# Two chained transformer blocks on one core: later norm statistics, halved conditioning products, plain float32 for the small heads

## The chip, the cores and the metric

The kernel runs on one core of a Trainium2 chip. The metric is device time in microseconds (us), smaller is better. A core has TensorE (PE; its weight loads are shown as PEld), VectorE (DVE), ScalarE (ACT), GpSimd (POOL), and SyncE (SP), which here only starts DMA transfers. Each engine runs its own instructions in order and waits on semaphores for the others.

## The reference, cut to what matters

Two blocks run one after the other on 256 tokens of width 1024. The first is a hybrid block of two layers on a latent and a context stream of 256 tokens each. Each layer begins with a conditioning vector: a product of one row per stream with `w_ada`, which scales and shifts the norm.

```
shift, scale, gate = split((silu(c) @ w_ada + b_ada), 3)      # and the same for the context
h = rmsnorm(x, norm_w) * (1 + scale) + shift
```

The second block also has two layers. Layer 0 mixes with `mixer_ab`, layer 1 with `mixer_cd`; both then do a cross-attention to a memory of 256 tokens and a gated feed-forward (`swiglu`, 2816 wide).

```
mixer_ab: qa, ka, va, qb, kb, vb = split(h @ w_in)       # 8 query heads, 2 key/value heads, 64 wide, twice
          a: rms_norm(q), rms_norm(k), rope, softmax(q k^T / 8) v
          b: rope, window mask, a sink column in the softmax
mixer_cd: c: compressed heads: q, k 64 + 32 wide, 8 heads, softmax(q k^T / sqrt(96)) v
          d: near heads: 8 heads, 64 wide, with a bias table and a column mask
every mixer, the cross-attention and the feed-forward read rms_norm(x) of the residual x
```

## The kernel before, in words

Activations lie feature-major, 128 features by 256 tokens per tile (`x[:, k]`, k from 0 to 7). A float32 operand is cut into a high and a low part in the reduced type fp32r (`split`, L266): ScalarE rounds (`copy`), VectorE subtracts. A product is then three matmuls (`mm3`, L258). Weights come as pieces of 128 x 1024 floats (512 KB) over SyncE's DMA queue into `w_raw` (three buffers), ScalarE makes `w_high`, and VectorE or GpSimd makes `w_low` (`split_into`, L250). Which of the two does it is set by the table `POOL` (L34): for each part of the program the first number says every how many pieces one goes to GpSimd, 0 for none. Ab has 1 (all), cd has 3.

Heads of 64 features use another form (`mm_stacked`): high and low parts of q are stacked over 128 rows, and k is laid twice, once high over high, once low over zeros (`stack_q`, `stack_k`), so a product is two matmuls. The softmax (`softmax_t`) takes scores of two heads in one PSUM bank: VectorE takes the maximum, ScalarE exponentiates and sums, VectorE scales (L1299), TensorE transposes, and the result is split into two parts again. `pair_values` (L1312) multiplies it with the values, three matmuls per product, 64 or 128 output rows.

The statistics of a norm: ScalarE squares each residual tile, GpSimd (VectorE for the last) sums the squares into `acc`. `rstd_cols` sums `acc` over the partitions with a matmul against ones (L347) and VectorE runs eleven small instructions for the inverse root (`rsqrt`, L331); `rstd_unit` lays the result along a row with two more products (L357) and a copy. The projections themselves read the unscaled tiles (`raw_norm`), and the factor is applied to their results. So the statistics are needed only behind a projection, though the program states them ahead of it.

The conditioning: `ada_product` (L502) computes 512 columns of one layer's row from eight pieces of k, loaded two at a time in four loads; each product has 32 output rows and takes one of four column groups of the array, and the second half of k is added onto the first in PSUM.

The order: the first block is traced inside a block that a planner schedules by a simulated timeline. The second block is ordered by the same framework by priority, which follows the order of the program, and by when operands are ready; so the order on an engine is not that of the lines. Loads are issued on SyncE in the order in which buffers come free. PSUM has eight banks: three `mm`, two `sc`, two `tp`, one `pv`.

## Time and profile before

| | us |
|---|---|
| median of 3 runs | 2439.83 (2437.66 to 2440.39) |
| the profiled execution | 2442.6 |
| its span | 2440.8 |
| TensorE busy in it | 2296.8 (94%) |
| VectorE busy | 1617.7 (66%) |
| ScalarE busy | 1163.4 (48%) |
| GpSimd busy | 472.2 (19%) |
| ab output projection, 1797 to 1829: TensorE busy | 31.7 of 32 |
| first feed-forward, 1878 to 2062: TensorE busy | 183.8 of 184 |
| second layer up to 2101, from 2062: TensorE busy | 36.0 of 39 |
| median from issue to landing of a 512 KB weight load | 3.4 |

Rows of the profile give times in us from the start of the span unless marked ns. A row of the order of time has the start, the duration, the engine, the line of the kernel, the operation, the tiles (out<-in), the shape and the count of what was merged; in brackets the idle time of the engine before it, and what ended it. A plain float32 matmul is recorded as two matmuls, a transpose or a reduced one as one. Matmuls are pipelined, so the distance of starts, and not the duration, tells what one takes of TensorE. PEclk is the granted clock as a share of full speed (2.4 GHz; the other level is 1.2 GHz).

The second block begins at about 1663 (mixer ab to 1829, with the memory's keys and values inside it, cross to 1867, feed-forward to 2062, mixer cd to 2200, cross, feed-forward to 2432).

### The profile page before, as it was taken

To read this page: it belongs to the slowest core of one execution; us is meant where nothing else is said; L and a number is where in the kernel's file an instruction comes from. 1 tells how busy PE (TensorE), PEld (TensorE's weight loads), DVE (VectorE), ACT (ScalarE), POOL (GpSimd) and SP (SyncE) were. 2 spreads that over 40 slices of the span, in tenths; PEclk is the share of its full clock that TensorE was granted. 3 is DMA by queue.
4 is the path that set the end of the run, shared out by engine and by line. 5 is a ranking of instruction groups with operands and counts; after the bars stand their busy time and mean duration, and the time that the engine had idled before them with its cause. 6 is when DMAs were issued, how large, how long until landed. Compare 5 with 4: busy or idle time off the path is not lost.

```text
span 2440.8 us, 40377 instructions
## 1 busy us (share of the span) xinstructions
PE 2296.8 (94%) x15566; PEld 2066.6 (85%) x15566; DVE 1617.7 (66%) x3372; ACT 1163.4 (48%) x2172; POOL 472.2 (19%) x354
## 2 busy tenths in 40 slices
PE   6999999999999999989999999898698999888998
PEld 3787878798797887779889999896588999788998
DVE  5745566466575555586557778666987766887765
ACT  3344443444554233335445666444465444665543
POOL 2422220111121102002110000123352211222221
PEclk8999999999999999999999999998899999999999
DMA  6223234323323434443445434554233555433554
GB/s 254 78 92 114 95 109 155 125 88 101 116 93 131 151 103 154 142 130 117 134 147 186 131 113 141 180 166 147 86 102 123 183 183 180 132 109 121 189 183 139
DMA packets 111072, 330.87 MB, mean 136 GB/s; under 512 B 12320, under 2 KB 24352, under 8 KB 110880
## 3 DMA queue, kind: packets, MB, share of 16 engines
q1 hardware_dynamic: 90432, 299.87, 37.5%
q10 hardware_dynamic: 20448, 28.42, 3.4%
q8 instruction: 123, 2.02, 0.4%
q14 instruction: 69, 0.57, 0.1%
HBM read 309.36 MB, written 18.87 MB: 134 GB/s over the span
## 4 chain that ended last, share of the span: by engine, by line
PE 80%; DVE 12%; ACT 3%; DMA 3%; issue 2%; POOL 0%; ACTq 0%; SPq 0%; DVEq 0%; POOLq 0%
PE mm L262 22%; PE mm L263 22%; PE mm L264 22%; PE pv L262 2%; PE pv L263 2%; PE pv L264 2%; DVE w_low L257 1%; DVE h L274 1%; ACT w_high L256 1%; DVE e L1299 1%; DMA w_raw<-wstream 1%; PE mm L510 1%; PE sc L303 1%; DVE mx L1279 1%; PE sc L304 1%
## 5 line engine op out<-in xcount | busy, mean ns | idle before, releaser
L256 ACT CAST w_high<-w_raw 128x1024 fp32r<-128x1024 f32 (+1 forms) x490 | 508.0, 1038 | 583.1 <-PE mm L263 351.8
L257 DVE TENSOR_TENSOR w_low<-w_raw,w_high 128x1024 fp32r<-128x1024 f32 (+1 forms) x395 | 497.3, 1260 | 189.3 <-ACT w_high L256 184.8
L262 PE MATMUL mm<-big,w_high 128*128 128x512 f32 (+1 forms) x1664 | 573.3, 346 | 12.4 <-DVE g L942 5.7
L263 PE MATMUL mm<-big,w_high 128*128 128x512 f32 (+1 forms) x1664 | 571.3, 344 | 0.0
L264 PE MATMUL mm<-big,w_low 128*128 128x512 f32 (+1 forms) x1664 | 570.0, 343 | 0.0
L257 POOL TENSOR_TENSOR w_low<-w_raw,w_high 128x1024 fp32r<-128x1024 f32 x95 | 230.4, 2428 | 739.6 <-ACT w_high L256 600.3
L262 PEld LDWEIGHTS mm<-big,w_high 128*128 128x128 f32 x1664 | 316.1, 190 | 56.6 <-DVE g L942 6.1
L264 PEld LDWEIGHTS mm<-big,w_low 128*128 128x128 f32 x1664 | 316.4, 190 | 37.5 <-DVE w_low L257 0.4
L263 PEld LDWEIGHTS mm<-big,w_high 128*128 128x128 f32 x1664 | 316.6, 190 | 36.5 <-DVE big L271 0.2
L263 PE MATMUL mm<-w_low,big 128*128 128x256 f32 x960 | 269.9, 282 | 4.2 <-POOL w_low L257 2.8
L262 PE MATMUL mm<-w_high,big 128*128 128x256 f32 x960 | 268.0, 282 | 1.6 <-ACT w_high L256 1.6
L264 PE MATMUL mm<-w_high,big 128*128 128x256 f32 x960 | 268.3, 281 | 0.0
L263 PE MATMUL mm<-h,w_high 128*128 128x256 f32 x896 | 255.5, 285 | 4.8 <-DVE h L274 4.1
L262 PE MATMUL mm<-h,w_high 128*128 128x256 f32 x896 | 253.4, 284 | 2.7 <-ACT h L273 1.7
L264 PE MATMUL mm<-h,w_low 128*128 128x256 f32 x896 | 253.6, 283 | 0.0
L263 PEld LDWEIGHTS mm<-w_low,big 128*128 128x128 f32 x960 | 181.1, 189 | 6.2 <-POOL w_low L257 3.7
L262 PEld LDWEIGHTS mm<-w_high,big 128*128 128x128 f32 x960 | 180.6, 189 | 3.5 <-ACT w_high L256 2.8
L264 PEld LDWEIGHTS mm<-w_high,big 128*128 128x128 f32 x960 | 181.0, 189 | 0.4
L263 PEld LDWEIGHTS mm<-h,w_high 128*128 128x128 f32 x896 | 169.7, 189 | 7.6 <-DVE h L274 7.5
L262 PEld LDWEIGHTS mm<-h,w_high 128*128 128x128 f32 x896 | 169.5, 190 | 4.4 <-ACT h L273 2.8
L264 PEld LDWEIGHTS mm<-h,w_low 128*128 128x128 f32 x896 | 169.7, 190 | 0.1
L1649 POOL TENSOR_TENSOR x<-x,r 128x256 f32<-128x256 f32 x44 | 60.2, 1368 | 190.7 <-ACT t L1648 190.7
(475 smaller groups left out, 4388.8 us busy)
## 6 DMA issues: line engine op xcount, KB each, us to landing
w_raw<-wstream SPq DMA_DIRECT2D x486, 512.0 KB, 3.4
w_raw<-wstream SPq DMA_DIRECT2D x32, 448.0 KB, 3.2
big<-wstream SPq DMA_DIRECT2D x16, 512.0 KB, 9.0
gates<-y ACTq DMA_DIRECT2D x24, 256.0 KB, 2.0
w<-gates SPq DMA_DIRECT2D x18, 256.0 KB, 3.8
load<-yacc ACTq DMA_DIRECT2D x16, 256.0 KB, 3.0
yacc<-w ACTq DMA_DIRECT2D x12, 256.0 KB, 2.0
gates<-y ACTq DMA_DIRECT2D x24, 128.0 KB, 1.8
```

Source lines behind the costliest of these rows:

```text
L256: nc.scalar.copy(h, raw)
L257: eng.tensor_tensor(lo, raw, h.bitcast(F32), op=ALU.subtract)
L262: nc.tensor.matmul(out, a[0], b[0], start=start, stop=False)
L263: nc.tensor.matmul(out, a[0], b[1], start=False, stop=False)
L264: nc.tensor.matmul(out, a[1], b[0], start=False, stop=stop)
L274: nc.vector.scalar_tensor_tensor(lo, src, scale, h.bitcast(F32), op0=ALU.mult, op1=ALU.subtract)
L303: nc.tensor.matmul(out, q, k[0], start=start, stop=False)
L304: nc.tensor.matmul(out, q, k[1], start=False, stop=stop)
L510: nc.tensor.matmul(ps[j:j + 32], self.sc32[:, 2 * q + k], raw[:, k], start=(q < 2), stop=(q >= 2))
L1279: nc.vector.reduce_max(mx, ps2, axis=AX.X, negate=True)
L1299: nc.vector.tensor_scalar(p[:, u], p[:, u], sm[:, u:u + 1], None, op0=ALU.mult)
L1649: nc.gpsimd.tensor_tensor(g, g, rb, op=ALU.mult)
```

## The change

- `POOL`: parts ab and cd give no weight split to GpSimd any more.
- The heads of 64 and of 96 features are computed in plain float32: queries and keys are copied once (keys into halves of tiles that are zero elsewhere, `make_zeroed_halves`, `key_tile`), probabilities are copied once, values are laid between zeros (`between_zeros`, two GpSimd memsets per tile), and the two heads of a pair add into one bank. A score product is one matmul instead of two or three, a value product one instead of three. The cross-attention keeps the three-matmul form.
- `rstd_cols` (and `rstd_unit`) stand behind the first projection of ab, cd, cross and feed-forward.
- The conditioning is made in two halves of k, one per head: four products after two loads, the last loaded one first and at high priority, the other three ordered behind it. The first half is copied to `acc`, the second added to it by VectorE.
- Tile counts follow: `act` 16 to 8, `p` 4 to 3, `vz` 4 new; the first eight feed-forward results use `vz`.

```diff
@@ -28,11 +28,11 @@
...
-SECOND = dict(load=2, act=16, q=8, p=4, x=4, e=3, s=2, t=3, r=2)
+SECOND = dict(load=2, act=8, vz=4, q=8, p=3, x=4, e=3, s=2, t=3, r=2)
...
-            merge0=(0, 0), merge1=(0, 0), t=(4, 2), e=(0, 0), ab=(1, 0), x=(3, 2), cd=(3, 1), f=(0, 0))
+            merge0=(0, 0), merge1=(0, 0), t=(4, 2), e=(0, 0), ab=(0, 0), x=(3, 2), cd=(0, 0), f=(0, 0))
@@ -296,6 +296,15 @@
...
+            self.zero_tiles.append(t)
+
+    def make_zeroed_halves(self, n):
+
+        self.zero_tiles, self.n_zero = [], 0
+        for i in range(n):
+            t = [self.pool.tile([P, S], F32, tag=f"kz{i}{u}", name=self.name("kz"), bufs=1) for u in range(2)]
+            for u in range(2):
+                self.nc.gpsimd.memset(t[u][64 * (1 - u):64 * (2 - u)], 0.0)
@@ -495,21 +504,26 @@
...
-    def ada_group(self, l, groups):
-        for g in groups:
-            self.ada_product(l, g)
-
-    def ada_product(self, l, g):
+    def ada_half(self, l, g, half):
...
-        for q in range(4):
-            raw = self.raw_weights("w_ada", l, 2 * q, 2, _cols(512 * g, 512)).rearrange("p (k c) -> p k c", k=2)
-            for k in range(2):
-                j = 32 * (2 * (q % 2) + k)
-                nc.tensor.matmul(ps[j:j + 32], self.sc32[:, 2 * q + k], raw[:, k], start=(q < 2), stop=(q >= 2))
+        raw = [self.raw_weights("w_ada", l, 4 * half + 2 * q, 2, _cols(512 * g, 512)).rearrange("p (k c) -> p k c", k=2) for q in range(2)]
+
+        def product(j):
+            return nc.tensor.matmul(ps[32 * j:32 * j + 32], self.sc32[:, 4 * half + j], raw[j // 2][:, j % 2], start=True, stop=True)
+
+
+        with self.tc.high_priority():
+            first = product(3)
+            with self.tc.issue_after(first.ins if hasattr(first, "ins") else first):
+                for j in range(3):
+                    product(j)
+        if half == 0:
+            nc.scalar.copy(self.acc, ps)
+            return
...
-        nc.scalar.copy(row, ps)
+        nc.vector.tensor_tensor(row, ps, self.acc, op=ALU.add)
@@ -676,8 +690,7 @@
...
-            if hd in (1, 3):
-                self.ada_group(l, range(4 + hd // 2, 5 + hd // 2))
+            self.ada_half(l, 4 + hd // 2, hd % 2)
@@ -689,9 +702,9 @@
...
+                if l == 0:
+                    self.ada_half(1, pair, u)
...
-            if l == 0:
-                self.ada_group(1, range(pair, pair + 1))
@@ -1300,7 +1313,9 @@
...
-        if whole:
+        if not isinstance(pts, tuple):
+            nc.scalar.copy(pts[:, :, :, sl], pt)
+        elif whole:
@@ -1309,16 +1324,28 @@
...
-    def pair_values(self, y, k, pts, vs):
-
-        po = self.bank("pv").rearrange("p (u c) -> p u c", u=2)
+    def between_zeros(self, n):
+
+        v = self.u("vz", [P, 64 * (2 * n + 1)])
+        self.nc.gpsimd.memset(v[:, :P * n].rearrange("p (g c) -> p g c", c=P)[:, :, :64], 0.0)
+        self.nc.gpsimd.memset(v[:, P * n:], 0.0)
+        return v, v[:, 64:].rearrange("p (g c) -> p g c", c=P)[:, :, :64]
+
+    def pair_values(self, y, k, pts, v, heads):
+
+        po = self.bank("pv")[:, :S]
...
-            m = 64 * (u + 1)
+            lo = P * heads[u] + 64 * (1 - u)
...
-                vh, vl = vs(u, s)
-                self.mm3(po[:m, u], (vh, vl), (pts[0][:, u, s], pts[1][:, u, s]), s == 0, s == 1)
-            rows = slice(64 * u, 64 * u + 64)
-            self.split(y[0][rows, k, :S], y[1][rows, k, :S], po[rows, u])
+                self.nc.tensor.matmul(po, v[s][:, lo:lo + P], pts[:, u, s], start=u == 0 and s == 0, stop=u == 1 and s == 1)
+        self.split(y[0][:, k, :S], y[1][:, k, :S], po)
+
+    def key_tile(self, src):
+
+        k = self.zeroed()
+        for u in range(2):
+            self.nc.scalar.copy(k[u][64 * u:64 * u + 64], src[64 * u:64 * u + 64])
+        return k
@@ -1366,37 +1393,32 @@
+        tab = {nm: self.cst(nm).rearrange("p (t c) -> p t c", t=2) for nm in ("r1_c", "r1_s", "r2_c", "r2_s")}
+
+        pss = self.tok_wide("w_in_ab_2", 0, h, AB_KV, self.early)
         r = self.rstd_cols(self.acc[:, :S], S, D)
-        tab = {nm: self.cst(nm).rearrange("p (t c) -> p t c", t=2) for nm in ("r1_c", "r1_s", "r2_c", "r2_s")}
-
-        pss = self.tok_wide("w_in_ab_2", 0, h, AB_KV, self.early)
...
-            v = tuple(self.u("act", dt=F32R) for _ in range(2))
-            vsrc = pss[t][:, 256:].rearrange("p (g c) -> p g c", c=64)
-            for dup in range(2):
-                o = [x.rearrange("p (g u c) -> p g u c", u=2, c=64)[:, :, dup] for x in v]
-                self.split(o[0], o[1], vsrc, scale=r[:, t:t + 1])
+            v, at = self.between_zeros(4)
+            nc.scalar.activation(at, pss[t][:, 256:].rearrange("p (g c) -> p g c", c=64), AF.Copy, scale=r[:, t:t + 1])
             vv.append(v)
...
+            kr = self.u("x")
+            kv = kr.rearrange("p (g u c) -> p g u c", u=2, c=64)
+            for i, (kx_, rn) in enumerate(((ka, "r2"), (kb, "r1"))):
+                self.rope_tok([kv[:, 2 * i + g, 0].unsqueeze(1) for g in range(2)], kx_, tab[rn + "_c"][:, t], tab[rn + "_s"][:, t], 2, 32)
+                nc.scalar.copy(kv[:, 2 * i:2 * i + 2, 1], kv[:, 2 * i:2 * i + 2, 0])
...
+        kT = [[self.key_tile(src[:, g * S:(g + 1) * S]) for g in range(2)] for src in (kt_ps, kt_ps2)]
@@ -1426,62 +1448,50 @@
-                qT[kind].append([self.u("q", dt=F32R) for _ in range(2)])
-                for u in range(2):
-                    self.stack_q(qT[kind][i][u], ptq[i][64 * u:64 * u + 64])
+                qT[kind].append(self.u("q"))
+                nc.scalar.copy(qT[kind][i], ptq[i])
...
-                        self.mm_stacked(ps[:, u], qT[kind][pr // 2][u][:, qsl], tuple(x[:, ksl] for x in kT[kind]), kind == 0, kind == 0 or u == 1)
+                        nc.tensor.matmul(ps[:, u], qT[kind][pr // 2][:, qsl], kT[kind][g][u], start=kind == 0, stop=kind == 0 or u == 1)
                     self.softmax_t(ps, pts, qi, sink=[x[:, 2 * pr:2 * pr + 2] for x in sink] if kind else None)
...
+            if j == 0:
+                q = self.u("q")[:, :S]
+                self.nc.vector.tensor_tensor(q, ps, rb, op=ALU.mult)
+            else:
+                k = self.zeroed()
+                for u in range(2):
+                    sl = slice(64 * u, 64 * u + 64)
+                    self.nc.vector.tensor_tensor(k[u][sl], ps[sl], rb[sl], op=ALU.mult)
+        return q, k
...
-        r = self.rstd_cols(self.acc[:, :S], S, D)
-        rb = self.rstd_unit(r)
@@ -1492,11 +1502,14 @@
...
                 ps = self.feat(w, 0, h, 0, S)
+                if lo == 0 and j == 0:
+                    r = self.rstd_cols(self.acc[:, :S], S, D)
+                    rb = self.rstd_unit(r)
                 nc.vector.tensor_tensor(raw[:, j], ps, rb, op=ALU.mult)
...
             rc = self.rstd_rows(acc, S, n * P, by=96.0 if n == 2 else 1.0)
-            c = tuple(self.u("p", [P, 2, S], F32R) for _ in range(2))
+            c = tuple(self.u("q", [P, 2, S], F32R) for _ in range(2))
             self.norm_gain(c, raw, rc, [self.vec(gain, k) for k in range(n)], "t")
@@ -1559,20 +1572,18 @@
...
-                a, b = (self.u("q", [P, 2, S], F32R)[:96] for _ in range(2))
-                self.split(a, b, pt)
-                pair.append((a, b))
-            pts = self.new_pts()
+                a = self.u("q", [P, 2, S])[:96]
+                nc.scalar.copy(a, pt)
+                pair.append(a)
+            pts = self.u("p", [P, 2, 2, S])
...
-                    a, b = pair[u]
-                    qsl = slice(qi * P, (qi + 1) * P)
-                    self.mm3(ps[:, u], (a[:, 0, qsl], b[:, 0, qsl]), (a[:, 1], b[:, 1]), True, True)
+                    nc.tensor.matmul(ps[:, u], pair[u][:, 0, qi * P:(qi + 1) * P], pair[u][:, 1], start=True, stop=True)
...
-            self.pair_values(y, pr, pts, lambda u, s, pr=pr: tuple(x[:, P * pr:P * pr + 64 * (u + 1)] for x in vc[s]))
-
-            pts = self.new_pts()
+            self.pair_values(y, pr, pts, vc, (2 * pr, 2 * pr + 1))
+
+            pts = self.u("p", [P, 2, 2, S])
@@ -1608,6 +1616,10 @@
+            if pr == 0:
+                r = self.rstd_cols(self.acc[:, :S], S, D)
+                rs = self.small("x_rs", [P, 2])
+                nc.vector.tensor_scalar(rs, r[:, :2], 128.0 ** -0.5, None, op0=ALU.mult)
@@ -1635,13 +1647,14 @@
...
-        rb = self.rstd_unit(self.rstd_cols(self.acc[:, :S], S, D))
...
+            if f == 0:
+                rb = self.rstd_unit(self.rstd_cols(self.acc[:, :S], S, D))
@@ -1649,7 +1662,9 @@
...
-            a = self.u("act" if f < 16 else "q", [P, 2, S], F32R)
+            if f % 2 == 0 and f < 8:
+                two = self.u("vz", [P, 2, 2, S], F32R)
+            a = two[:, f % 2] if f < 8 else self.u("act" if f < 16 else "q", [P, 2, S], F32R)
...
```

## Rows read from the trace of the kernel before

**Rows 1.** The stretches of time: start:end, length, busy time and count per engine, PEclk, DMA.
```profile
0.00:1663.00 1663.00, 1589.73 (x10236) 1398.58 (x10236) 1053.24 (x2363) 755.87 (x1402) 270.64 (x222) 0.99 0.40 132
1663.00:1740.00 77.00, 56.43 (x223) 44.17 (x223) 56.34 (x125) 30.93 (x53) 28.99 (x12) 0.80 0.37 124
1740.00:1797.00 57.00, 45.11 (x291) 39.24 (x291) 53.17 (x128) 37.56 (x113) 16.75 (x8) 0.94 0.18 56
...
2101.00:2176.00 75.00, 62.65 (x442) 56.24 (x442) 64.25 (x125) 57.96 (x152) 17.27 (x14) 0.93 0.37 120
```

**Rows 2.** TensorE's waits from 1663 to 1740: total us, times, longest.
```profile
PE tp L1426 <- DVE x L1337: 7.7, 2, 7.5
PE tp L1394 <- DVE x L1337: 4.9, 1, 4.9
...
PE tp L347 <- DVE acc L379: 2.7, 1, 2.7
```

**Rows 3.** TensorE's waits from 1740 to 1797.
```profile
PE tp L1301 <- DVE e L1299: 8.2, 7, 1.9
```

**Rows 4.** VectorE in order of time, in the first key norm of ab.
```profile
1681.78 0.16 DVE L337 SCALAR_TENSOR_TENSOR hn_r_t<-hn_r_y 128x2 f32<-128x2 f32 x1
1681.97 2.36 DVE L338 TENSOR_TENSOR hn_r_t<-hn_r_t,hn_r_v 128x2 f32<-128x2 f32 x1
```

**Rows 5.** GpSimd in order of time: memsets ahead of ab, and one weight split.
```profile
1641.47 1.92 POOL L298 MEMSET kz<- 64x512 f32 x4
...
1681.95 2.37 POOL L257 TENSOR_TENSOR w_low<-w_raw,w_high 128x1024 fp32r<-128x1024 f32 x1 [0.43 <-ACT w_high L256]
```

**Rows 6.** Groups on GpSimd from 1663 to 1829: count, busy us, mean ns, idle before.
```profile
L257 POOL TENSOR_TENSOR w_low<-w_raw,w_high 128x1024 fp32r<-128x1024 f32 x26 | 62.4, 2403 | 98.6 <-ACT w_high L256 89.3 <-DMA load<-rpb 5.6 <-PE pv L264 3.8
```

**Rows 7.** Groups on VectorE from 1663 to 1829.
```profile
L1299 DVE TENSOR_SCALAR e<-e,sm 128x256 f32<-128x256 f32 x32 | 20.1, 663 | 0.2
L274 DVE SCALAR_TENSOR_TENSOR h<-xres,vecs,h 128x256 fp32r<-128x256 f32 x15 | 17.9, 1225 | 3.9 <-ACT h L273 3.9
...
L271 DVE TENSOR_TENSOR p<-tp,p 128x512 fp32r<-128x512 f32 x16 | 10.7, 682 | 1.4 <-ACT p L270 1.3
L338 DVE TENSOR_TENSOR hn_r_t<-hn_r_t,hn_r_v 128x8 f32<-128x8 f32 x6 | 7.5, 1252 | 0.2
```

**Rows 8.** Groups on VectorE from 2062 to 2200.
```profile
L257 DVE TENSOR_TENSOR w_low<-w_raw,w_high 128x1024 fp32r<-128x1024 f32 x17 | 22.1, 1298 | 3.2 <-ACT w_high L256 3.1
```

**Rows 9.** TensorE in order of time: two reduced matmuls of 256 columns.
```profile
1745.24 0.28 PE L303 MATMUL sc<-act,q 128*128 128x256 f32 x1
1745.36 0.28 PE L304 MATMUL sc<-kz,q 128*128 128x256 f32 x1
```

**Rows 10.** TensorE in order of time, the statistics in the first feed-forward.
```profile
1874.55 0.55 PE L347 MATMUL tp<-ones,acc 128*128 128x2 f32 x4
...
1878.43 0.68 PE L357 MATMUL tp<-ident,rstd 128*128 128x128 f32 x4 [0.16 <-DVE rstd L339]
1878.86 0.36 PE L263 MATMUL mm<-h,w_high 128*128 128x256 f32 x1
```

**Rows 11.** Groups on TensorE from 2101 to 2176.
```profile
L1301 PE MATMUL tp<-ident,e 128*128 128x128 f32 x64 | 12.0, 304 | 6.1 <-DVE e L1299 5.9
```

**Rows 12.** TensorE in order of time, conditioning products of two groups.
```profile
216.49 1.91 PE L510 MATMUL mm<-w_raw,sc 128*32 128x512 f32 x12
...
221.72 1.05 PE L510 MATMUL mm<-w_raw,sc 128*32 128x512 f32 x4 [1.02 <-DMA w_raw<-wstream]
...
470.06 1.06 PE L510 MATMUL mm<-w_raw,sc 128*32 128x512 f32 x8
471.05 0.38 PE L347 MATMUL tp<-ones,e 128*128 128x2 f32 x2
```

**Rows 13.** What ended TensorE's idle time ahead of line 510, in total: us, times.
```profile
  DMA w_raw<-wstream: 9.2, 9
```

More of the change, by code (lines that the diff above doesn't have):

```diff
@@ L415, in run @@
                 self.bufs, self.banks = SECOND, BANKS_2
-                self.make_zeroed(4)
+                self.make_zeroed_halves(4)
                 self.load_consts(CUT_2, self.pool, "consts")
@@ L1387, in mixer_ab @@
             self.head_norm(ka, 2, self.vec("g_ka"))
-            kr = self.u("x")[:, :256]
-            kv = kr.rearrange("p (g c) -> p g c", c=64)
-            self.rope_tok(kv[:, 0:2], ka, tab["r2_c"][:, t], tab["r2_s"][:, t], 2, 32)
-            self.rope_tok(kv[:, 2:4], kb, tab["r1_c"][:, t], tab["r1_s"][:, t], 2, 32)
-            for g in range(4):
-                nc.tensor.transpose((kt_ps, kt_ps2)[g // 2][:64, (g % 2) * S + t * P:(g % 2) * S + (t + 1) * P], kv[:, g], self.ident)
-        kT = []
-        for src in (kt_ps, kt_ps2):
-            k = self.u("act", dt=F32R), self.zeroed()
-            self.stack_k(k, src[:64])
-            kT.append(k)
+            kr = self.u("x")
[3 more added lines that the diff above has]
+                nc.scalar.copy(kv[:, 2 * i:2 * i + 2, 1], kv[:, 2 * i:2 * i + 2, 0])
+            for g in range(4):
+                nc.tensor.transpose((kt_ps, kt_ps2)[g // 2][:, (g % 2) * S + t * P:(g % 2) * S + (t + 1) * P], kr[:, P * g:P * g + P], self.ident)
+        kT = [[self.key_tile(src[:, g * S:(g + 1) * S]) for g in range(2)] for src in (kt_ps, kt_ps2)]
         y = self.new_y2()
@@ L1442, in mixer_ab @@
                     for u in range(2):
-                        self.mm_stacked(ps[:, u], qT[kind][pr // 2][u][:, qsl], tuple(x[:, ksl] for x in kT[kind]), kind == 0, kind == 0 or u == 1)
+                        nc.tensor.matmul(ps[:, u], qT[kind][pr // 2][:, qsl], kT[kind][g][u], start=kind == 0, stop=kind == 0 or u == 1)
                     self.softmax_t(ps, pts, qi, sink=[x[:, 2 * pr:2 * pr + 2] for x in sink] if kind else None)
-                def vs(u, s, g=g, kind=kind):
-                    lo = (2 * kind + g) * P
-                    return tuple(x[:, lo:lo + 64 * (u + 1)] for x in vv[s])
-                self.pair_values(y, 4 * kind + pr, pts, vs)
+                self.pair_values(y, 4 * kind + pr, pts, vv, (2 * kind + g,) * 2)
         self.memory_now(l)
@@ L1454, in near_project @@
     def near_project(self, pr, rb):
-        qk = []
         for j in range(2):
@@ L1459, in near_project @@
             ps = self.feat(w, 0, self.h, 0, S)
-            t = self.u("x")[:, :S]
-            self.nc.vector.tensor_tensor(t, ps, rb, op=ALU.mult)
-            for u in range(2):
-                if j == 0:
-                    q = self.u("q", dt=F32R)[:, :S]
-                    self.stack_q(q, t[64 * u:64 * u + 64])
-                    qk.append(q)
-                else:
-                    k = self.u("q", dt=F32R)[:, :S], self.zeroed()[:, :S]
-                    self.stack_k(k, t[64 * u:64 * u + 64])
-                    qk.append(k)
-        return qk
+            if j == 0:
[7 more added lines that the diff above has]
+        return q, k
     def mixer_cd(self, l):
@@ L1476, in mixer_cd @@
         self.share("cd")
-        r = self.rstd_cols(self.acc[:, :S], S, D)
-        rb = self.rstd_unit(r)
         def values():
@@ L1482, in values @@
             for t in range(2):
-                v = tuple(self.u("act", dt=F32R) for _ in range(2))
-                self.split(v[0], v[1], pss[t], scale=r[:, t:t + 1])
+                v, at = self.between_zeros(8)
+                nc.scalar.activation(at, pss[t].rearrange("p (g c) -> p g c", c=64), AF.Copy, scale=r[:, t:t + 1])
                 vd.append(v)
@@ L1549, in mixer_cd @@
             self.tok(ps, [(wv, 1)], ckv, t * P)
-            v = tuple(self.u("act", dt=F32R) for _ in range(2))
-            self.split(v[0], v[1], ps)
+            v, at = self.between_zeros(8)
+            nc.scalar.copy(at, ps.rearrange("p (g c) -> p g c", c=64))
             vc.append(v)
@@ L1568, in mixer_cd @@
                 for u in range(2):
[L1569 to L1571 removed]
+                    nc.tensor.matmul(ps[:, u], pair[u][:, 0, qi * P:(qi + 1) * P], pair[u][:, 1], start=True, stop=True)
                 self.softmax_t(ps, pts, qi)
[L1573 to L1575 removed]
+            self.pair_values(y, pr, pts, vc, (2 * pr, 2 * pr + 1))
+            pts = self.u("p", [P, 2, 2, S])
             for qi in range(2):
@@ L1584, in mixer_cd @@
                 for u in range(2):
-                    self.mm_stacked(ps[:, u * S:(u + 1) * S], qk[u][:, qi * P:(qi + 1) * P], qk[2 + u])
+                    nc.tensor.matmul(ps[:, u * S:(u + 1) * S], qk[0][:, qi * P:(qi + 1) * P], qk[1][u], start=True, stop=True)
                 nc.vector.scalar_tensor_tensor(s2, ps, 0.125, bias, op0=ALU.mult, op1=ALU.add)
                 self.softmax_t(s2.rearrange("p (u c) -> p u c", u=2), pts, qi)
-            self.pair_values(y, 4 + pr, pts, lambda u, s, pr=pr: tuple(x[:, P * pr:P * pr + 64 * (u + 1)] for x in vd[s]))
+            self.pair_values(y, 4 + pr, pts, vd, (2 * pr, 2 * pr + 1))
             if pr < 3:
@@ L1610, in cross @@
                 qs.append((a, b))
+            if pr == 0:
+                r = self.rstd_cols(self.acc[:, :S], S, D)
+                rs = self.small("x_rs", [P, 2])
+                nc.vector.tensor_scalar(rs, r[:, :2], 128.0 ** -0.5, None, op0=ALU.mult)
             pts = self.new_pts()
```

5 lines of the change are left out of this document (removed).

## The prediction

> **What bounds the kernel now.** I read the page first (the table above): TensorE is busy 2296.8 of 2440.8 us, VectorE 66%, which leaves 144 us in which TensorE is idle. The stretches of time say where [rows 1]: the first block (0 to 1663) is idle 73 us out of 1663, and the feed-forward stages of the second are full (183.8 of 184 us). The idle time sits in the ab mixer: 20.6 us of 77 before its attention (1663 to 1740), there also at a granted clock of 0.80 of full speed, and 11.9 of 57 in its attention; and in the cd mixer: 12.4 of 75 in its attention. So these stages are limited by what feeds TensorE, and the rest by TensorE itself.
>
> The list of waits names the feeder: before the ab attention TensorE waits 7.7 and 4.9 us for VectorE's rope and 2.7 us for the last sum of squares [rows 2]; in the attention 8.2 us for VectorE's scaling of the exponentials [rows 3]. VectorE is not only busy there, it is held: of two instructions of the same two columns one takes 0.16 us and the next 2.36 us, from 1681.97 to 1684.33, while GpSimd's weight split runs from 1681.95 to 1684.32 [rows 4, 5]. The pattern repeats: the 26 splits on GpSimd in the ab mixer take 2.40 us each [rows 6], and four groups of VectorE have means far above their shortest: the 32 scalings of 256 columns mean 663 ns, the 15 h splits 1225 ns [rows 7], where half of a p split of 512 columns (682 ns [rows 7]) would be 341; hn_r_t, 6 of 8 columns and 6 of 2, means 1252 [rows 7] against 0.16 [rows 4]. The excess: 32 x 0.32 = 10.3; 15 x 0.75 = 11.2, taking 0.48 as the h split's own time; 12 x 1.08 = 13.0. Some 35 us of VectorE are held time.
>
> **POOL table: ab and cd to (0, 0).** The splits move to VectorE. One took 1.30 us there in the cd mixer (a mean of 17, some held as well [rows 8]); I cost it at 1.15, four times the 256-column scaling's 0.34 less what back-to-back instructions overlap, and 1.30 is the other bound (4 us more in ab, off the path by the sums below). Ab: 25 x 1.15 = 28.8 us added, 35 us of holding gone. Cd, where every third weight goes to GpSimd (8 of them): 9.2 added.
>
> The Trainium skill (SBUF — State Buffer, section "SBUF: two separate sides") states that VectorE and GpSimd share one pair of ports under an exclusive lock, kept for the whole instruction; the rows above agree (2.36 against 2.37 us [rows 4, 5]). By that rule the twelve memsets that the change adds on GpSimd could hold VectorE as well, at 0.48 us each (a fourth of the nearest row, 1.92 for four [rows 5]) an estimated 5.8 us, and the sum below would be 2405. No row shows a memset holding VectorE, and I leave it out.
>
> **Plain float32 heads.** VectorE and ScalarE lose the low halves. VectorE in ab: the 16 splits of p, 10.7 us [rows 7]; the others go by the same row, 0.68 for 512 columns and 0.4 for 256: 8 of the 16 of y (3.2), 8 of q (5.5), two of kz and four of v (3). Together 22, so VectorE's net over the ab mixer is -22 - 35 + 29 = -28 us. In cd 16 of p, 8 of y, 8 of q from the transposes, 16 of 256 columns for near q and k (8 take their place, 4 net of the product they replace), 4 of v: 11 + 3 + 5.5 + 5 + 3 = 27 us less, 9 more.
> TensorE pays. A reduced-float32 matmul of 256 columns starts 0.12 us after the one before [rows 9]. A plain one of 128 columns shows as two recorded matmuls: four of them (two products) hold TensorE from 1878.43 to 1878.86, so 0.43 us for 2 x 128 columns, and 0.43 for one of 256 [rows 10]. A group (a pair of heads, one kind) has 4 products for scores and 4 for values, 8 x 0.43 = 3.44. Before: 8 + 12 reduced ones, 20 x 0.118 = 2.36 (ab and the near heads), or 12 + 12 = 2.83 (compressed heads). More: 1.08 x 8 = 8.6 us in ab; 1.08 x 4 + 0.61 x 4 = 6.8 in cd.
>
> *Ab before the attention* (77 us). Upper end: busy 56.4 us, which at full clock would be 0.80 x 56.4 = 45, so 32 us could go. Lower end: only what VectorE loses in this stretch: the holding of hn_r_t (13.0) and half of q, kz and v (4 of 8.5) less the 12 weight splits that GpSimd does here (13.8), 3. I take 20, nearer the upper end, because TensorE's waits on the chain (7.7 + 4.9) and the low clock that follows them are this row, while the weight splits need not lie in the chain: TensorE takes 12 matmuls of 512 columns, 2.8 us, per split. The start's 2.7 us is in the 20, and its price too: the statistics' matmul goes behind the key and value projection, so the eleven VectorE instructions that follow it (11 x 0.2 = 2.2 us), and the scaling of the keys that is queued behind them, can come that much later; the two cancel. Bounds 3 and 32.
> *Ab attention* (57 us). At full clock 0.94 x 45.1 = 42.4, plus 8.6 is 51, so at most 6 gained; at worst the 8.6 is all lost. I take a gain of 5: VectorE falls from 53 busy to some 35 (14 of the p splits and half of y, 12; half of q, 3; the scalings' holding, 10; plus 6 weight splits, 7), and what TensorE waits for now, 8.2 us [rows 3], has room to go. The output projection (1797 to 1829) is full already (table above): nothing. Ab: -25.
> *Cd*. To 2101 3 us idle, in the attention 75 - 0.93 x 62.7 - 6.8 = 10 at best, 6.8 lost at worst. I take -6 and -1 for the two stretches, since the scaling alone keeps TensorE waiting 5.9 us there [rows 11] and VectorE, at 64 of 75, loses 18: -7.
>
> **Statistics behind the first projection.** The program order is not what runs: the scheduler already puts the sum's matmul among the projection's (1874.55, no wait before it [rows 10]) and the row broadcast after it, with 0.16 us of wait. So in cross and cd this changes nothing (-0.5 to +0.5 each). In ffn it can cost: at 1878.43 the broadcast stands right behind the first pair of projections; placed after them, sum and chain (3.9 us from 1874.55 to 1878.43) start some 2.5 us later. Three mm banks cover one more projection, 24 x 0.118 = 2.8 us; then TensorE waits for the first gate's bank, about 1 us per layer. Bounds -1 to +2.5 each. I take +2 for both, -1 for the two cross stages: +1.
>
> **Conditioning in halves** (first block). Now a group of 8 products has 4 loads; only three raw buffers exist, so the fourth load starts when TensorE has freed one and lands 3.4 us later (table above). It shows as 12 + 4 recorded matmuls, 1.91 and 1.05 us, in pairs of column groups [rows 12]. Over the 8 groups TensorE waits 9.2 us for these loads [rows 13]. After: 16 halves of 4 products in four column groups at once, the x8 row, 0.99 us (470.06 to 471.05 [rows 12]): 15.8 us instead of 8 x (1.91 + 1.05) = 23.7 less 1 for the overlap at their ends, so -6.9. Waits: a half needs two buffers, not four, so one stays for the stream; I take away half of the 9.2 and add 1.5 for the eight extra switches: -10 (-6.9 - 4.6 + 1.5). Bounds: nothing (the plan of this block is new everywhere, and its idle 73 us can shift), and -18 (all the waits and the refill of the split weights behind them). Against: the buffer rival below. The smaller tile counts (act 8, p 3) cost nothing: cross, the only stage that still takes p in pairs, is through with its first pair's values before the second pair's splits begin; were it not, one value product of 24 x 0.12 = 3 us would be waited for in each of two stages.
>
> **Sum.** -25 - 7 + 1 - 10 = -41 us on the profiled span of 2440.8, 2399.8; that execution took 2442.6, 1.8 outside the span, and lies 2.8 above the median of 2439.83. On the median: **2399 us**.
>
> **Rivals.**
> *A, deeper gain*: every reachable wait goes. Ab -32 - 6, cd -13, ada -18, statistics 0: -69, 2371. For it: all of it is the same holding, and TensorE has projections to fill with. Against: the score, softmax, transpose, value chain stays.
> *B, TensorE takes VectorE's place*: the float32 columns all lie on the path, +15.4. Waits on VectorE go (-12.6 before the attention, -8.2 and -5.9 in the two [rows 2, 3, 11]), ada gives nothing, statistics +3: -8, 2432. For it: cd's attention is 84% busy [rows 1]. Against: ab has 32 us of slack ahead of it [rows 1].
> *C, slower*: the 16 halves at high priority wait in TensorE's in-order queue for the second of their two loads. A load takes 3.4 us to land; 16 x 3.4 = 54 us, less the 9.2 now waited and the 6.9 saved: +38. With -31 from the rest: +7, 2447. It decides from 2.9 us of wait per half ((31 + 16) / 16). Against: now the wait per group is 1.1 us (9.2 / 8), because other products are found for TensorE meanwhile.
> *D, no effect*: the scheduler makes up all that was moved, and the holding is idle time that something else fills; 2440. For it: the statistics are such a case. Against: TensorE visibly waits.
>
> **Chances.** Forecast 0.55 (2385 to 2415), A 0.20, B 0.15, C 0.05, D 0.05. Range: 2364, a little beyond A, to 2432, B. Under 0.2% (5 us) this kernel's runs (2437.66 to 2440.39) can't tell a change from none. Faster 0.90, same 0.05, slower 0.05.
>
> **What would show it.** GpSimd's splits gone from ab and cd, and no VectorE instruction of two columns above 0.3 us there; the ab stretch (first projection to the end of its output) at some 141 us instead of 166, clock above 0.9; plain products at 0.43 us; cd at 131 instead of 138; 16 visits of 0.99 us for the conditioning without waits over 1 us. Wrong would be: VectorE's chain unchanged in length, TensorE full but longer in the attentions (B), or waits on loads before the conditioning's products (C).

## The result, and the profile after

The changed kernel takes 2381.73 us (2377.26 to 2387.68, four runs) against 2439.7 for the kernel before; the ratio is 0.9765, with an interval of 0.9741 to 0.979. Run again beside two of the experiments it took 2378.36 (ratio 0.9763, 0.9744 to 0.9781). The forecast was 2399, within 2364 to 2432: 41 us less, where 58 came.

The profiled execution has a span of 2375.5 us, 65.3 below the one of before. First the busy times of the whole page, then stretches of time of the changed kernel (start:end, length, busy time and count for PE, PEld, DVE, ACT, POOL, the granted clock, DMA).

```profile
PE 2278.8 (96%) x15486; PEld 2056.9 (87%) x15486; DVE 1560.4 (66%) x3332; ACT 1145.0 (48%) x2134; POOL 401.3 (17%) x336
```

```profile
0.00:1631.00 1631.00, 1573.74 (x10236) 1392.32 (x10236) 1051.14 (x2371) 755.68 (x1403) 277.74 (x230) 0.99 0.41 134
1631.00:1698.00 67.00, 54.91 (x235) 43.27 (x236) 51.34 (x141) 33.67 (x66) 3.80 (x2) 0.82 0.47 157
1698.00:1738.00 40.00, 39.28 (x225) 33.07 (x224) 29.35 (x96) 27.60 (x91) 0.00 (x0) 1.00 0.08 27
1738.00:1780.00 42.00, 41.99 (x300) 39.21 (x299) 28.41 (x35) 23.07 (x36) 9.22 (x8) 1.00 0.50 163
2043.00:2110.00 67.00, 64.57 (x411) 56.85 (x410) 42.26 (x87) 48.68 (x129) 8.68 (x6) 1.00 0.41 134
```

Read beside [rows 1]: the first block, where no line of the mixers runs, is 32 us shorter, and its idle time falls from 73 to 57 us. The cd attention (2043 to 2110 now) is 67 us where it was 75, at full clock and with 2.4 us idle instead of 12.4. For ab the cuts differ a little from those of [rows 1]; at the same landmarks (the first and the last transposes of exponentials, and the end of the output projection) the kernel before has

```profile
1663.00:1743.00 80.00, 58.63 (x233) 46.26 (x234) 59.21 (x132) 33.76 (x62) 28.99 (x12) 0.80 0.35 119
1743.00:1798.00 55.00, 43.75 (x289) 37.84 (x288) 51.27 (x124) 34.84 (x104) 16.75 (x8) 0.95 0.19 59
1798.00:1831.00 33.00, 32.04 (x251) 30.56 (x250) 24.33 (x26) 19.49 (x32) 24.39 (x14) 1.00 0.49 158
```

so the part ahead of the attention lost 13 us, and attention and output projection together 6 (55 + 33 against 40 + 42: projections of the memory that filled the attention before now run behind it). Ahead of the attention the clock is still low: 0.82 over the stretch, at half from 1676 to 1693, behind one wait of TensorE for rope and around a second one (3.8 us up to 1674.9, 4.8 up to 1689.6). TensorE's waits from 1631 to 1780 (total us, times, longest):

```profile
PE tp L1448 <- DVE x L1364: 8.6, 2, 4.8
PE tp L356 <- DVE acc L388: 2.7, 1, 2.7
...
PE tp L1314 <- DVE e L1312: 0.3, 1, 0.3
```

The wait for the scaled exponentials, 8.2 us in [rows 3], is down to 0.3. The waits for rope, 7.7 and 4.9 in [rows 2], are still 8.6 in sum, and the one for the last sum of squares is the same 2.7: moved behind the projection in the program, the sum's matmul runs first in ab all the same. Groups on VectorE in the same stretch (count, busy us, mean ns), the answer to [rows 7]:

```profile
L257 DVE TENSOR_TENSOR w_low<-w_raw,w_high 128x1024 fp32r<-128x1024 f32 x27 | 33.2, 1231 | 14.0 <-ACT w_high L256 13.8
L274 DVE SCALAR_TENSOR_TENSOR h<-xres,vecs,h 128x256 fp32r<-128x256 f32 x16 | 11.4, 745 | 0.8 <-ACT h L273 0.8
...
L1312 DVE TENSOR_SCALAR e<-e,sm 128x256 f32<-128x256 f32 x32 | 10.0, 349 | 0.4
...
L347 DVE TENSOR_TENSOR hn_r_t<-hn_r_t,hn_r_v 128x2 f32<-128x2 f32 (+1 forms) x12 | 2.0, 163 | 0.3
```

The small products of the key norm, two and eight columns together, were before

```profile
L338 DVE TENSOR_TENSOR hn_r_t<-hn_r_t,hn_r_v 128x2 f32<-128x2 f32 (+1 forms) x12 | 14.9, 1244 | 0.4
```

The scalings mean 349 ns instead of 663, these small products 163 instead of 1244, the h splits 745 instead of 1225, and a weight split takes VectorE 1.23 us.

### The profile page after: what moved, and what is told of

The parts are those of the page before. It is cut to its first block, busy times and chain, and to the rows that moved or that the text cites. A ratio compares the mean times of both kernels' runs of the same rounds, so it can differ in the third digit from the quotient of the medians.

```text
span 2375.5 us, 40130 instructions
## 1 busy us (share of the span) xinstructions
PE 2278.8 (96%) x15486; PEld 2056.9 (87%) x15486; DVE 1560.4 (66%) x3332; ACT 1145.0 (48%) x2134; POOL 401.3 (17%) x336
## 5 line engine op out<-in xcount | busy, mean ns | idle before, releaser
L257 DVE TENSOR_TENSOR w_low<-w_raw,w_high 128x1024 fp32r<-128x1024 f32 (+1 forms) x429 | 533.9, 1245 | 225.9 <-ACT w_high L256 222.3
L257 POOL TENSOR_TENSOR w_low<-w_raw,w_high 128x1024 fp32r<-128x1024 f32 x61 | 148.9, 2443 | 526.8 <-ACT w_high L256 441.7
L905 POOL TENSOR_TENSOR e<-e,s 128x256 f32<-128x256 f32 (+3 forms) x68 | 64.7, 964 | 180.9 <-ACT e L904 180.7
```

The costliest lines, as they stand in the source:

```text
L257: eng.tensor_tensor(lo, raw, h.bitcast(F32), op=ALU.subtract)
L905: nc.gpsimd.tensor_tensor(e, e, place(sc, s, lo, hi), op=ALU.mult)
```

## Experiments

Every experiment computes the whole reference. "First block" is the time to the sum of squares that opens ab, in the profiled execution, and the time at 1.2 GHz is what the clock's record has in it:

```
                        median us   first block   idle in it   of it at 1.2 GHz
before                  2439.7      1663.2        73.4         47.8
splits only             2407.39     1662.6        73.1         47.8
heads only              2425.43     1657.0        72.3         37.5
halves only             2410.61     1636.2        58.8         47.8
halves together         2422.98     1648.6        67.3         54.6
halves, plain order     2410.68     1636.5        56.2         44.4
halves, two groups      2428.38     1652.8        55.1         41.0
changed                 2381.73     1630.8        57.1         37.5
changed, again          2378.36     1633.4        58.9         37.5
```

The stages of the second block, from one stage's sum-of-squares matmul to the next, in us (only kernels in which these matmuls stand at the old place, so that the landmarks are the same):

```
                        ab      cross   feed-fwd   cd      cross   feed-fwd
before                  167.7   43.5    188.6      137.4   44.4    187.1
splits only             144.2   42.3    188.6      131.2   42.2    187.1
heads only              166.6   43.6    188.3      127.0   43.1    186.8
changed, stats back     147.9   42.3    188.3      124.2   42.3    186.8
```

**Conditioning in halves alone** (the kernel before, with `ada_half` and its calls):

```diff
-            if hd in (1, 3):
-                self.ada_group(l, range(4 + hd // 2, 5 + hd // 2))
+            self.ada_half(l, 4 + hd // 2, hd % 2)
...
-            if l == 0:
-                self.ada_group(1, range(pair, pair + 1))
+                if l == 0:
+                    self.ada_half(1, pair, u)
```

> The kernel before with only the conditioning in halves. In the two traces the first block is 32.3 us shorter (1663.4 to 1631.1 us), where the prediction gave the halves 10. Theory 1: the halves cause all of it, since nothing else in that block was edited: 32 us less than before, 2408, ratio 0.987. Theory 2: the halves are worth the predicted 10, and the other 22 us are a chance of this one execution or come from the second block's changed tiles: 2430, ratio 0.996. The second block must stay at its 777 us by either.

2410.61 us (2408.3 to 2413.68), ratio 0.9894 (0.987 to 0.9917): 25 us less than the 2435.89 of before beside it. Theory 2 is out. Theory 1's 32 is too much, and the table says by how much: of the executions with 47.8 us at 1.2 GHz, the two without halves (before, splits only) are 26.4 to 27 us above the one with halves only in the first block; of those with 37.5, heads only is 24 to 26 above changed; between the two groups lie 3 to 6 us, for 10 us more at half the clock. Of the 32.3 us between the two profiles some 26 are the halves, and the rest is where the low stretches fell in these two executions.

Where the 26 are: idle time in the block falls by 14.6 us (73.4 to 58.8). What the products hold TensorE for (from the start of the matmul ahead of a visit to the start of the one behind it, less idle time) falls from 27.6 to 20.9, by 6.7. The last 5 are spread over the block's other matmuls in the new order; they stay open. Most of the idle time that went belongs to the weight stream. These are TensorE's waits for weights and loads from 95 us to the end of the block, first before, then with halves only:

```profile
PE mm L262 <- ACT w_high L256: 5.1, 7, 1.6
PE mm L510 <- DMA w_raw<-wstream: 3.9, 4, 1.6
PE mm L263 <- POOL w_low L257: 2.8, 2, 1.6
PE mm L263 <- DVE w_low L257: 1.2, 2, 0.7
```

```profile
PE mm L262 <- ACT w_high L256: 2.1, 5, 0.7
PE mm L263 <- DVE w_low L257: 0.5, 1, 0.5
```

13.0 us against 2.6. Only 3.9 of the 13.0 stand ahead of the conditioning's own products; the others are ordinary projections whose split weights are not there yet, and 7.2 of those 9.1 us stand within 10 us behind the last product of a group (at 340, 572, 576, 665, 758 and 1189). Between two weight casts on ScalarE lie 26 to 29 us at five of the groups before (539.42 to 568.76 at one); from 300 to 760 with halves only, at most 15.

**Both halves at the group's old place** (halves, but called one behind the other):

```diff
-            self.ada_half(l, 4 + hd // 2, hd % 2)
+            if hd in (1, 3):
+                for half in range(2):
+                    self.ada_half(l, 4 + hd // 2, half)
```

> The kernel before with the conditioning in halves, but both halves of a group one behind the other at the group's old place in the program. The halves at their own places gave 25 us (2411 against 2436). Theory S (spacing: four loads in a row for one group hold the weight stream up, two do not): together they are four loads in a row again, only the TensorE term of 7 us is left: 2429, ratio 0.997. Theory M (form: four products at once, with no group that waits half done for its fourth load): the gain stays at 20 or more: 2414, ratio 0.991.

2422.98 us (2419.05 to 2427.66), ratio 0.9933 (0.9914 to 0.9952): 14.5 us less than before, some 10 to 12 short of the halves at their own places, so by the time between the two theories. The waits for weights and loads from 95 us on are in between as well, 6.0 us:

```profile
PE mm L262 <- ACT w_high L256: 2.3, 5, 0.9
PE mm L263 <- DVE w_low L257: 2.1, 3, 0.8
PE mm L264 <- DVE w_low L257: 1.1, 1, 1.1
PE mm L505 <- DMA w_raw<-wstream: 0.5, 2, 0.3
```

That is 3.4 us more than with the halves apart, of 8.5 us more idle time. Most of the rest is another wait: the transposes of line 1163 wait 7.7 us for the scaled exponentials, where with the halves apart they wait 0.6. Three of these waits stand a few us behind a group, and there VectorE is held as in [rows 4, 5]. GpSimd, VectorE and TensorE at one of them (an instruction of four columns takes 2.35 us beside GpSimd's weight split; at 652 and 743 it is the same, 2.29 and 2.32):

```profile
560.61 2.36 POOL L257 TENSOR_TENSOR w_low<-w_raw,w_high 128x1024 fp32r<-128x1024 f32 x1 [27.87 <-DVE b_rs_y L335]
560.64 2.35 DVE L337 SCALAR_TENSOR_TENSOR b_rs_t<-b_rs_y 128x4 f32<-128x4 f32 x1
564.40 0.41 PE L1163 MATMUL tp<-ident,e 128*128 128x128 f32 x2 [2.49 <-DVE e L1160]
```

So the 10 to 12 us are only in part the four loads in a row: the wait for weights has some 3 of them, and where the splits on GpSimd fall some 7. No run parts the two, and theories S and M are not settled by this one.

**Halves in plain order** (no priority for the first product):

```diff
-        with self.tc.high_priority():
-            first = product(3)
-            with self.tc.issue_after(first.ins if hasattr(first, "ins") else first):
-                for j in range(3):
-                    product(j)
+        for j in range(4):
+            product(j)
```

> The kernel before with the conditioning in halves at their new places, without the priority of the first product and the order behind it: four products in program order. Theory S and theory M both leave the gain as it was, 25 us: 2411, ratio 0.990. Theory P (the priority, by which the products of one half come as one visit, carries the gain): the products stand apart and take 2 visits of 0.99 us each, and half of the gain goes: 2424, ratio 0.995.

2410.68 us (2405.83 to 2411.96), ratio 0.9885 (0.9868 to 0.9901): the same as with the priority. Theory P is out, although its mechanism is seen: six of the sixteen halves come in two visits. TensorE in order of time, one such half:

```profile
289.61 1.05 PE L505 MATMUL mm<-w_raw,sc 128*32 128x512 f32 x2
290.59 0.39 PE L262 MATMUL pv<-v,w 128*128 128x258 f32 x1
...
291.14 1.06 PE L505 MATMUL mm<-w_raw,sc 128*32 128x512 f32 x6
292.13 0.50 PE L262 MATMUL sc<-q,k 128*128 128x512 f32 x1
```

The six extra visits of about 1 us show as 5.8 us more of TensorE (from the start of a visit to that of the next matmul, in sum 21.7 against 15.9), and the idle time is 2.6 lower.

**Halves in two column groups** (as the last, but two products are added to the two before):

```diff
-            return nc.tensor.matmul(ps[32 * j:32 * j + 32], ..., start=True, stop=True)
+            return nc.tensor.matmul(ps[32 * (j % 2):32 * (j % 2) + 32], ..., start=j < 2, stop=j >= 2)
```

> As the run with halves in plain order, but the four products of a half go into two column groups, two of them added to the two before, so a half takes TensorE about 2 us instead of 1. Sixteen halves, 16 us more on TensorE: if its time in this block counts in full (the first block is 97 per cent busy) 2427, ratio 0.996. If the halves' gain is in waits and the products lie beside other waits: 2411 to 2415, ratio 0.990 to 0.992.

2428.38 us (2427.53 to 2430.86), ratio 0.9964 (0.9951 to 0.9977): 17.7 us more than the run in plain order, for 16 forecast. A half now holds TensorE from 1178.07 to 1179.91:

```profile
1178.07 1.91 PE L505 MATMUL mm<-w_raw,sc 128*32 128x512 f32 x8
1179.91 0.39 PE L262 MATMUL sc<-q,k 128*128 128x256 f32 x1
```

The first block is 16.3 us longer (table), so TensorE's time there counts in full, and the 6.7 us that the form saves may be taken to count as well.

**Weight splits of ab and cd on VectorE alone** (the kernel before):

```diff
-... ab=(1, 0), x=(3, 2), cd=(3, 1), f=(0, 0))
+... ab=(0, 0), x=(3, 2), cd=(0, 0), f=(0, 0))
```

> The kernel before with only the weight splits of the ab and cd mixers taken from GpSimd to VectorE. Theory H (held port): VectorE was held by GpSimd's splits, so this alone gives most of the 37 us that ab and cd lost between the traces: 25 us less, 2415, ratio 0.990, and no two-column VectorE instruction above 0.3 us in ab. Theory W (work): the split work that VectorE takes over (about 29 us in ab, 9 in cd) eats what the holding gives back: within 5 us of before, ratio 0.998 to 1.002; the gain then needs the low halves gone.

2407.39 us (2405.2 to 2412.17), ratio 0.9885 (0.9865 to 0.9906): 28.5 us less, theory H. Ab loses 23.5 us and cd 6.2 (table). The low halves are all still there, and the scalings and small products are not held any more (groups on VectorE in ab):

```profile
L1299 DVE TENSOR_SCALAR e<-e,sm 128x256 f32<-128x256 f32 x32 | 10.0, 346 | 0.1
...
L338 DVE TENSOR_TENSOR hn_r_t<-hn_r_t,hn_r_v 128x2 f32<-128x2 f32 (+1 forms) x12 | 1.9, 162 | 0.3
```

**Plain float32 heads alone** (the changed kernel with GpSimd's splits, the groups and the statistics as before):

```diff
-... ab=(0, 0), x=(3, 2), cd=(0, 0), f=(0, 0))
+... ab=(1, 0), x=(3, 2), cd=(3, 1), f=(0, 0))
...
-            self.ada_half(l, 4 + hd // 2, hd % 2)
+            if hd in (1, 3):
+                self.ada_group(l, range(4 + hd // 2, 5 + hd // 2))
...
+        r = self.rstd_cols(self.acc[:, :S], S, D)      # ahead of the projection, in all four stages
```

> The kernel before with only the small heads in plain float32 (GpSimd keeps its weight splits, conditioning and statistics are as before). Theory H: VectorE stays held, TensorE pays 15 us for the wider products, and VectorE's shorter queue brings some 20: 5 us less, 2435, ratio 0.998. Theory W: VectorE's work is what TensorE waits for, 49 us of it go: 25 us less, 2415, ratio 0.990.

2425.43 us (2419.89 to 2430.08, nine runs), ratio 0.9954 (0.994 to 0.9968): 10.5 us less, between the theories, and by stages nothing in ab (-1.1 us) and 10.4 in cd. In ab VectorE is still held, with less work around it:

```profile
L1308 DVE TENSOR_SCALAR e<-e,sm 128x256 f32<-128x256 f32 x32 | 12.0, 410 | 0.4
L347 DVE TENSOR_TENSOR hn_r_t<-hn_r_t,hn_r_v 128x2 f32<-128x2 f32 (+1 forms) x12 | 8.5, 710 | 0.4
```

**Statistics back at their old place** (the changed kernel otherwise; shown for the feed-forward stage, likewise in ab, cd and cross):

```diff
+        rb = self.rstd_unit(self.rstd_cols(self.acc[:, :S], S, D))
...
-            if f == 0:
-                rb = self.rstd_unit(self.rstd_cols(self.acc[:, :S], S, D))
```

> The changed kernel with only the statistics at their old place, ahead of each stage's first projection. Theory 1 (the moved statistics cost what the two cross and two feed-forward stages are longer, 0.9 + 2.2 + 1.0 us and about 1 of the first feed-forward): 4 us less than the changed kernel, 2378, ratio to before 0.975. Theory 2 (the prediction's +1, at the edge of what can be told): 2381, ratio 0.976. Theory 3 (the move pays in ab and cd, by letting the first projection start before the last sum of squares is there): 2386 to 2390, ratio 0.978 to 0.980.

2376.21 us (2374.5 to 2380.07), ratio 0.9757 (0.9738 to 0.9776). Theory 3 is out; the first two can't be told apart by the medians, 0.9757 against 0.9763 to 0.9765. This kernel's stages beside those of the run with the splits only (table) show what the heads do once the splits are gone from GpSimd: 3.7 us more in ab (144.2 to 147.9), 7.0 less in cd (131.2 to 124.2). Windows of ab's attention up to the output projection, splits only and then this kernel, say what pays:

```profile
1724.00:1778.00 54.00, 49.70 (x333) 43.34 (x333) 51.47 (x137) 40.04 (x118) 0.00 (x0) 0.98 0.13 43
```

```profile
1693.00:1754.00 61.00, 60.28 (x326) 50.51 (x326) 40.57 (x116) 37.32 (x111) 0.00 (x0) 0.98 0.13 44
```

With plain heads VectorE has 11 us less and TensorE 10.6 more, in a stretch that is 7 us longer and full.

**Feed-forward statistics back, and the heads of ab too**, beside the changed kernel:

> The changed kernel again, beside the two runs below on one chip, as their measure: ratio to before 0.9765, as it was.

2378.36 us (2374.78 to 2379.76). The run beside it, with the feed-forward statistics back:

```diff
+        rb = self.rstd_unit(self.rstd_cols(self.acc[:, :S], S, D))      # in ffn alone, ahead of the loop
```

> The changed kernel with only the feed-forward stages' statistics ahead of their first projection; ab, cd and cross keep them behind it. By the two traces, matmul for matmul, the move cost 2.5 us at the first feed-forward stage and 2.2 to 3.5 at the second, and gave 0.7 in ab, 0.7 in cd and 1.1 to 1.6 in each cross stage: 5 us less than the changed kernel, 2377 where that has 2382. If these differences are the clock's alone: no difference.

2376.4 us (2371.82 to 2382.43), ratio 0.975 (0.973 to 0.9769): 2 us less, not to be told from none. Matmul for matmul against this run's profile, the changed kernel loses at the start of the first and of the second feed-forward stage 2.0 and 3.5 us in its first profile, 3.5 and 2.9 in the one taken beside this run. Its rows at the first (first profile, TensorE in order of time):

```profile
1821.35 0.50 PE L356 MATMUL tp<-ones,acc 128*128 128x2 f32 x4
...
1825.18 0.68 PE L366 MATMUL tp<-ident,rstd 128*128 128x128 f32 x4 [0.39 <-DVE rstd L348]
1827.41 0.38 PE L262 MATMUL mm<-h,w_high 128*128 128x256 f32 x1 [1.55 <-DVE x L1660]
```

Chain and broadcast come later than the banks reach, and TensorE waits 1.55 us for the first gate's bank, where before the broadcast was followed by the next projection at once [rows 10].

The last run has, besides, the heads of ab in three products again:

```diff
-                pts = self.u("p", [P, 2, 2, S])
+                pts = self.new_pts()
...
-                        nc.tensor.matmul(ps[:, u], qT[kind][pr // 2][:, qsl], kT[kind][g][u], ...)
+                        self.mm_stacked(ps[:, u], qT[kind][pr // 2][u][:, qsl], tuple(x[:, ksl] for x in kT[kind]), ...)
...
-                self.pair_values(y, 4 * kind + pr, pts, vv, (2 * kind + g,) * 2)
+                self.pair_values3(y, 4 * kind + pr, pts, vs)      # the old pair_values; ab's q, k, v split as before
```

> As the run with the feed-forward statistics back, and with the heads of ab (not those of cd) as three products of rounded high and low parts again, GpSimd without splits there. With the splits gone from GpSimd, ab took 144.2 us with the old heads and 148.0 with plain ones, cd 131.2 and 124.2. Theory T (in ab TensorE is what the heads are paid with, 8.6 us of wider products): 4 us less than the run above, 2373. Theory V (VectorE still bounds ab's attention, and the stage's difference is the clock's): 5 us more than the run above.

2368.93 us (2367.94 to 2370.23), ratio 0.9726 (0.9709 to 0.9744): 7.5 us below the run above and 9.4 below the changed kernel on the same chip. All four executions lie below all five of the run above. Theory T: in ab the plain heads cost. Ab takes 146.5 us in its profile, against 151.2 in that of the run above and 149.5 in both of the changed kernel, which has the same ab. From the first transposes of exponentials to the end of the output projection, the run above and then this one:

```profile
1707.50:1784.00 76.50, 75.79 (x478) 67.06 (x478) 54.01 (x126) 47.52 (x122) 7.47 (x7) 1.00 0.27 86
1700.00:1771.50 71.50, 66.62 (x483) 59.65 (x482) 65.27 (x153) 49.91 (x130) 7.69 (x7) 1.00 0.28 92
```

The 5 us lie there, at full clock in both, so they are not the clock's (theory V): TensorE has 9.2 us less to do and VectorE 11.3 more. As the forecast was 4 us, part of the 7.5 may be the wide spread of the run above. This version is the fastest of all that ran.

## Why the prediction was right or wrong

Measured parts, alone: halves 25.3, splits 28.5, heads 10.5, together 64.3 us; all three at once (statistics back) 59.7. The 4.6 us between are about what the intervals leave open, but the stages (table) show that splits and heads overlap: one by one they take 23.5 and 1.1 us from ab and 6.2 and 10.4 from cd, together 19.8 and 13.2. Of the 17 us by which the forecast was short, the halves are 16; what ab gave less than forecast (5) and cd more (6) cancels, which is luck.

**Where the idle time is** was read too narrowly. "The idle time sits in the ab mixer" is true of its share, not of its sum: the first block, "idle 73 us out of 1663", has half of all the idle time, and the largest error was made there.

**Conditioning in halves: the term that was mis-sized**, -10 for some -26. Its TensorE part was right (-6.9 forecast, -6.7 measured). The failing step was the waits: "Over the 8 groups TensorE waits 9.2 us for these loads" and "I take away half of the 9.2". The 9.2 of [rows 13] is itself a double count: line 510 has weight loads and matmuls, each with its own idle time, and the nine waits are 3.9 us ahead of matmuls (four) and 5.3 ahead of weight loads (five), four of them at the same moments. All of the 3.9 went (the changed kernel has no wait for a load ahead of L514), so the 4.6 that the sum took for this place came near it by luck, from too large a wait and too small a share. What the sum put at nothing stood elsewhere: while four loads go to one group, no weights come to be split, and ordinary projections wait, for w_high and w_low, 9.1 us before and 2.6 with halves only; other waits in the block fell by 4 more. The lower bound, -18, named this refill and was still short of the sum; 5 us of the 26 are unexplained. The rows that would have shown it were in the trace, as waits of other lines.

**Splits to VectorE**: the step held. The holding of 10.3 and 13.0 us that was read out of the means of [rows 7] is gone (20.1 to 10.0, and 14.9 to 1.9 over both shapes), a split costs 1.23 (1.15 to 1.30 forecast). Of the 11.2 us put down to the h splits only some 7 were holding: they still mean 742 ns with the splits alone and 745 in the changed kernel, where the prediction took 0.48 us as their own time. Small groups that it did not list make up for it (the h splits of loaded tiles, for one, go from 5.9 to 3.7 us), so its 35 us in all is near, in part by luck. Worth 29 us by itself, it is the largest part of the change, in ab above all.

**Ab**, -25 forecast, 20 measured (167.7 to 147.9, in the run with the statistics back, where the landmarks are the same). "I take 20, nearer the upper end" for the part ahead of the attention was 13: TensorE still waits 8.6 us for the rope chain, of 12.6, and the clock stays at 0.82, where above 0.9 was forecast. "I take a gain of 5" for the attention came as 6 or 7 with the output projection, but from the splits; over the whole stage the heads took 4 back. The price of 8.6 us on TensorE was right in size (9.2 in the last run), its cover was not there: four products of values start at 1705.27 and the next matmul at 1707.10, 0.46 us each, for 0.43 forecast.

**Cd**, -7 forecast, 13 measured (137.4 to 124.2). The mechanism was right and two sizes were off: "I take -6 and -1 for the two stretches" came as 8 in the attention (75 to 67, near the "10 at best") and some 4 ahead of it, where the prediction names 3 us of idle time. Here the heads pay, 7 us beyond the splits: with the splits alone the stage still had waits for the scaled exponentials, for the low halves of p and for y; in the changed kernel it has 1.8 us for the exponentials and 0.9 besides.

**Statistics**, +1 forecast: by the traces about +6 in the two feed-forward stages, and some 1 us back in each other stage, as far as the clock lets that be told; by the medians 2 us, not told from none. The mechanism was as forecast, down to the wait for the first gate's bank.

**Rivals.** A (2371) was right for cd (-13), nearer than the forecast for the halves (-18 of -26), and wrong in ab (-38 for -20); the time lies between the forecast and A. B's mechanism, TensorE in VectorE's place, is real in ab's attention and nowhere else. C is out: no half waits for its load; its price per group, 1.1 us, rests on the same double count. Of the signs, the splits, the plain products and the sixteen visits came as told, ab at 141 us and its clock above 0.9 did not; one visit and its neighbours in the changed kernel, for [rows 12]:

```profile
141.01 0.40 PE L262 MATMUL mm<-big,w_high 128*128 128x512 f32 x1
141.33 1.07 PE L514 MATMUL mm<-w_raw,sc 128*32 128x512 f32 x8
142.33 0.50 PE L263 MATMUL mm<-big,w_high 128*128 128x512 f32 x1
```

## What to carry to other kernels

A side product's burst of loads is paid for by whoever waits for the stream behind it: look for its price in the waits of other lines, spread the loads, and count the idle time of a block in sum, not in share. When several engines' work changes at once, price each part with the others already in place: plain float32 heads paid in cd, where VectorE was the limit, and cost 4 to 8 us in ab once the splits had freed VectorE. And ask whether the same fault stands in other stages: in the first block of the changed kernel 22 VectorE instructions of at most eight columns still take 0.6 to 2.3 us each, 28.9 us in sum, all beside a GpSimd operation; no run takes that block's splits from GpSimd. Two executions of one plan can differ by 6 us in where the clock is low, so a difference of two profiles is checked against a third.

## What the hardware showed that was not expected

Where they met, memsets on GpSimd did not hold VectorE. The prediction had an estimate of 5.8 us for that, kept out of its sum. In cd of the changed kernel, GpSimd and then VectorE in order of time:

```profile
1999.25 0.53 POOL L1330 MEMSET vz<- 128x512 f32 x1 [5.96 <-PE mm L264]
```

```profile
1999.38 1.09 DVE L257 TENSOR_TENSOR w_low<-w_raw,w_high 128x896 fp32r<-128x896 f32 x1 [0.43 <-ACT w_high L256]
```

The split that starts inside the memset takes its usual 1.09 us for 896 columns (1.23 for 1024). The Trainium skill (SBUF — State Buffer, section "SBUF: two separate sides") limits the lock for a VectorE operation with two inputs in SBUF to GpSimd operations that read SBUF, which a memset does not; the trace agrees, and the prediction had applied the rule without that condition.

A visit of conditioning products holds TensorE for about 1 us whether it has one product (289.61 to 290.59, two recorded matmuls) or four in four column groups (141.33 to 142.33, eight).
